# Two orders of the SBUF pools in a two-layer diffusion trunk step: the activation halves below or above the weights

## The chip, the cores and the metric

One core of a Trainium2 chip runs the whole program. The metric is the device time of one execution in microseconds: 2422.73 us before the change, the median of three runs (2418.14, 2423.43 and 2422.73).

## What is computed

The reference is one inference step of a trunk of two layers, of width 2048, over two groups of 128 tokens each (a prompt and a sample). They are computed side by side, 256 columns wide. Cut to what matters here:

```
for l in range(2):
    xp = xp + gp1 * mixer(modulate(xp, ...))     # l = 0: attention and convolution; l = 1: S5 and GQA
    xs = xs + gs1 * mixer(modulate(xs, ...))
    a  = relu(modulate(x, ...) @ w1[l])          # 2048 -> 8192
    x  = x + g2 * (a * a) @ w2[l]                # 8192 -> 2048, for both groups
y = rms_norm(x, final_norm)
```

All is float32. The shifts, scales and gates come from a modulation, which is a linear of two conditioning vectors by `ada_w`.

## The kernel before

**A linear.** Activations stand with features on the partitions: a tile `X[k]` holds 128 features of all 256 tokens. An output tile `lin` of 128 features is a sum over 16 such tiles (or another number of them). Weights arrive by DMA in pieces of 128 rows by 1024 (512 KB, 4,096 bytes on each partition) in the pool `raw` of 8 slots. ScalarE casts a piece to fp32r into `wh`, and VectorE writes what the cast lost, `raw - wh`, into `wl`; both pools have 4 slots of the piece's size. Activations are split in the same way: `put` writes the cast into the first half of a tile `hl`, and what it lost into the second half.

One piece of weights serves 8 tiles `X[k]`. For each of them `block` issues three matmuls of 256 columns: `wh` by the first half, `wh` by the second half, `wl` by the first half. So a **part** (the function `part`) is 24 matmuls, each with a weight load of its own, and a linear of 16 tiles is two parts, 48 matmuls.

**The MLP.** Both layers run the 8192 hidden features in four chunks of 16 tiles. A chunk's up stage is 16 linears by `w1` that read the 16 tiles of the modulated norm; its down stage is 16 linears by `w2` that read the chunk's 16 hidden tiles. Layer 1 runs the stages in the order up 0, up 1, down 0, down 1, up 2, down 2, up 3, down 3; layer 0 runs up and down by turns. After each up linear ScalarE writes `ms` and VectorE `mq` (the squared relu); after each down linear VectorE adds two halves to `x`. These rows mark the ends of linears in a timeline.

**Where activation halves lie.** Tiles named `hl` come from two pools. `hlp` (pool "hl", 24 slots, opened in `setup`) holds 516 numbers to a tile, 2,064 bytes, since one kind of its tiles carries two more columns; the built program sets its slots 2,080 bytes apart. `hp` (pool "hid") is opened by `mlp`, after everything in `setup`; its tiles hold 512 numbers and stand 2,048 bytes apart. Of a chunk's 16 hidden tiles the first 8 are in `hid` and the last 8 in `hlp`, except in chunk 1 of layer 1, where all 16 are in `hid`. So a down linear reads a part from `hid` and then a part from `hlp`, and an up linear reads two parts from `hlp`.

Slots of `hlp` are taken as they come free. In the built program the last part of an up linear reads slots 16, 15, 14, 13, 12, 11, 10, 9 in this order in both layers. The `hlp` part of a down linear reads 8, 1, 2, 3, 4, 5, 6, 7 in layer 0 and 12, 11, 10, 9, 4, 5, 6, 7 in layer 1.

**What sets the order.** The program is written as many strands. A first run keeps a clock for each engine and picks the order; the second builds the program in that order. The clocks don't know addresses. Loads go out on SP's queue as far ahead as `raw` has room; pieces of the modulation (`ada`, TensorE by `raw` itself, and `va` on VectorE) are woven in between.

**Where pools lie.** Pools are stacked in the order in which `setup` opens them, and the stage pools (`hid` and those of the mixers) come on top. The sum of the sizes below the stage pools is the same in either order, so stage pools don't move.

Of the kernel before, what the change touches and what calls it, by code (L numbers as in the profile page):

```python
# [48 lines left out]
class Engine:  # L49
    """An engine whose instructions are also charged to the program's clocks."""  # L50
# [27 lines left out]
class Line:  # L78
    """A strand of the program: a generator that says what its next instructions wait for."""
# [4 lines left out]
    def on_pe(self):  # L84
        """Whether its next instructions are for TensorE."""
        return callable(self.wait) and getattr(self.wait, "pe", False)
# [25 lines left out]
class Kern:  # L112
# [20 lines left out]
    # The program is many strands. A first run, that is thrown away, keeps a clock for each engine and always goes  # L133
    # on with a strand whose operands are there by then; the second run builds the program in that order, with
    # the weights loaded and split ahead of their use.
# [59 lines left out]
    def at(self, *aps):  # L195
        """When the tiles' contents are there."""
        return max([0] + [NEVER if v.tensor.name in self.held else self.at_.get(v.tensor.name, 0) for v in aps])

    def hold(self, t):
        """Not all of t is written yet."""  # L200
        self.held[t.tensor.name] = True
# [10 lines left out]
    def bulk(self, lead):  # L212
        """For work that is not urgent: the engines have come up to `lead` behind the clock of TensorE."""
        return lambda: max(self.clock["vector"], self.clock["scalar"]) + lead
# [58 lines left out]
    def get(self, *tags, on=None):  # L273
        """Waits for free slots (and for tiles), and takes them."""
        def ok():
            for t in set(tags):
                if self.live.get(t, 0) + tags.count(t) > self.cap[t]:
                    return False
            return self.when(on) + (MARGIN if "ps" in tags else 0)
        ok.pe = "ps" in tags  # L280
        yield ok
        for t in tags:
            self.live[t] = self.live.get(t, 0) + 1
# [10 lines left out]
    def setup(self):  # L294
        nc = self.nc
        self.const = self.pool("const", 1)
        self.xp = self.pool("xres", 1)
        self.hlp = self.pool("hl", 24)
        self.rawp = self.pool("raw", RAW)
        self.whp = self.pool("wh", SPLIT + 1)  # L300
        self.wlp = self.pool("wl", SPLIT + 1)
        self.work = self.pool("work", 2)
        self.ps = self.pool("ps", 1, PSUM)
        self.dram = self.pool("dram", 1, DRAM)
        pk = self.const.tile([128, _width(PACK)], F32, name="pk")
        nc.gpsimd.dma_start(pk, self.i["pack"])
        self.pk = {k: pk[:, a:b] for k, (a, b) in PACK.items()}
        self.x = self.xp.tile([128, KT, 256], F32, name="x")
        for q in range(2):
            nc.sync.dma_start(self.x[:, 8 * q:8 * q + 8], self.i["xT"][:, 8 * q:8 * q + 8])  # L310
        self.ones = self.const.tile([128, 128], F32, name="ones")
        nc.vector.memset(self.ones, 1.0)
        self.eps = self.const.tile([128, 1], F32, name="eps")
        nc.vector.memset(self.eps, EPS)
        self.ident = self.pk["ident"]
        self.condp = self.const.tile([128, KT, 32], F32, name="condp")
        nc.vector.memset(self.condp, 0.0)
        nc.scalar.activation(self.condp[:, :, 0:2], self.pk["cond"].rearrange("p (k c) -> p k c", c=2), AF.Silu)
        self.pick2 = self.const.tile([128, 2, 32], F32, name="pick2")
        nc.vector.memset(self.pick2, 0.0)  # L320
        for c in range(2):
            nc.vector.memset(self.pick2[:, c, c:c + 1], 1.0)
        self.mod, self.A, self.set_up = {}, {}, True
# [6 lines left out]
    def source(self, spec):  # L330
        """The columns of a piece, side by side."""
# [38 lines left out]
    def pump(self, upto=0):  # L370
        """Loads ahead, as far as there is room, and splits what has come (and the pieces before `upto` in any
        case)."""
# [24 lines left out]
    def slot(self, key, bufs, back=0):  # L397
        """When the slot of the next tile (or one after it) is free."""
        ring = self.rings.get(key, [])
        i = len(ring) + back - bufs  # L400
        return self.last.get(ring[i], (0, 0))[0] if 0 <= i < len(ring) else 0

    def peek(self, n, split=False):
        """When the next n raw tiles are there."""
# [5 lines left out]
    def take(self, split, *spec):  # L410
        """The next piece that has been loaded: its halves, or itself."""
# [32 lines left out]
    def there(self, X, a, b, weights=True):  # L444
        """For a wait: the tiles X[a:b], and the weights that come next."""
# [14 lines left out]
    def part(self, ps, src, X, a, b, first, last, w=None, **kw):  # L460
        """ps (+)= weight blocks a to b of a tile times X[a:b]."""
# [20 lines left out]
    def staged(self, srcs, X, width, groups, done, release=None):  # L482
        """Linears in groups: first all on the half of X that is there first."""
        n = 0
        for g in groups:
            # the first weights come before the banks are free
# [15 lines left out]
    def pairs(self, srcs, X, tags, done, cuts, between=None):  # L502
        """Linears side by side, two to a bank (of the given tags): first all on the part of X that is there first.
        done(n, ps, release) takes the tiles; between() is issued after the first part."""
# [16 lines left out]
        for i, (a, b) in enumerate(cuts):  # L521
            last = i == len(cuts) - 1
            # at the end one of each bank first: its copy out holds the bank
            for n in list(range(0, len(out), 2)) + list(range(1, len(out), 2)) if last else range(len(out)):
                ps, r = out[n]
                # the start of the first tile of a bank clears all of it
# [6 lines left out]
    def out_proj(self, src, X, done, held, between=None):  # L533
        """The tiles of an output projection, whose second half of X is there first."""
# [8 lines left out]
    def put(self, X, k, src, pool=None, slot=False):  # L543
        """X[k] = the halves of src."""
# [12 lines left out]
    def copied(self, dst, ps, note=None, release=None):  # L557
        """dst = ps, a linear's tile."""
# [10 lines left out]
    def ada(self, *pieces):  # L569
        """Two pieces (l, i, a, b) of the modulation: blocks a to b of vector i."""  # L570
# [44 lines left out]
    def ada_vector(self, n, pool):  # L615
        """Pieces of the modulation on VectorE, when it has time; TensorE only sums over the partitions."""
# [24 lines left out]
    def background(self):  # L641
        """The modulation in the order of its use: first parts of shift and scale, then theirs second."""
# [7 lines left out]
    def cuts(self, l, j):  # L650
        """The parts in which a modulated norm comes."""
        return FIRST if (l, j) == (0, 0) else ((0, 8), (8, 16))

    def mods(self, *keys):
        """For a wait: pieces of the modulation."""
        return lambda: self.at(*[self.mod[k] for k in keys]) if all(k in self.mod for k in keys) else False

# [1 line left out]
    def rstd_rows(self, sums, n, width, tag):  # L659
        """rstd of the sums in sums[:, :n] (token on the partition)."""  # L660
# [12 lines left out]
    def rstd_bcast(self, acc, width):  # L673
        """acc [128, 256]: squares summed over tiles; the rstd of each token on all partitions."""
# [20 lines left out]
    def sq_start(self, *norm):  # L695
        """The next norm's sum begins, and what doesn't wait for it."""
# [25 lines left out]
    def scales(self, l, j, a, b):  # L722
        """The factor of the modulated norm, with its gain."""
# [18 lines left out]
    # The first linears of a modulated norm don't wait for the sum over all of x: W (rstd A x + B) is  # L742
    # rstd (W A x) + W B, and B comes along as two more columns.
# [25 lines left out]
    def enter(self, l, j, srcs, groups, done):  # L769
        """The modulated norm of x; done(n, v, release) takes the first linears."""  # L770
# [36 lines left out]
    def residual(self, k, ps, l, i, summed, release=None, final=False):  # L807
        """x += gate * ps; the squares of the new x go to the next norm's sum if it has begun."""
# [17 lines left out]
    def softmax_parts(self, ps_list, scales, pool, tag, ebufs=2):  # L826
        """exp of the scaled scores (each a [128, 384] bank: prompt | sample) and the sums, per part."""
# [24 lines left out]
    def rope(self, out, src, rot, cos, sin, n, pool, tag, **kw):  # L852
        """out = src * cos + rot * sin for [128, n, 128] views."""
# [116 lines left out]
    def conv(self, gates, cins, cv, csum, mp, m2, mix):  # L970
# [21 lines left out]
        # layer norm of the convolution, silu  # L992
# [45 lines left out]
    def norm_heads(self, heads, ssq, ats, sub, m2, mix, hds):  # L1038
        """rms norm of the heads."""
# [206 lines left out]
    def gqa_scales(self, g, qss, qn, rqs, m2):  # L1246
        """The scale of each token's scores: rstd of the query, over sqrt(dim)."""
# [62 lines left out]
    def cmul(self, out_r, out_i, ar, ai, br, bi, tmp, neg_i=False):  # L1310
        """out = a * b, complex; tmp gives two scratch views of out's shape."""
# [13 lines left out]
    def s5_powers(self, kk, q1, z):  # L1325
# [4 lines left out]
        with ExitStack() as st:  # L1330
# [16 lines left out]
            # reduced angle: th - 2 pi n, with the product split so that it is exact  # L1347
# [33 lines left out]
            # k = (abar - 1) / a  # L1381
# [16 lines left out]
            # orders of powers: q1 for the chunk's state (7 - s | s), z for its output (i | 8 - i)  # L1398
# [111 lines left out]
    def s5(self, uts, mp, m2, fin, yhl):  # L1510
        """Two halves of the channels; the second one's states are prepared while the first one's are scanned."""
# [6 lines left out]
    def s5_states(self, qh, uts, mp, m2, out):  # L1518
        nc = self.nc
        u4 = range(4 * qh, 4 * qh + 4)  # L1520
        # u by (position in the chunk, channel) on the partition
# [29 lines left out]
        # states that each chunk adds  # L1551
# [38 lines left out]
    def s5_outputs(self, qh, u2, hs, mp, m2, fin, yhl):  # L1590
        nc = self.nc
        tt = nc.gpsimd.tensor_tensor
        # recurrence over the chunks (the backward half runs from the last)
# [22 lines left out]
        # outputs  # L1616
# [155 lines left out]
    def fill(self, most, goal, parts):  # L1772
        """How far the modulation pieces may run (in steps), and how far they have to within that many parts."""
# [47 lines left out]
def _channels():  # L1821
    """Order of the S5 channels: tile (qh, g4), partition (q', n)."""
# [101 lines left out]
```

## Time and profile before

| | |
|---|---|
| runs | 2418.14, 2422.73, 2423.43 us |
| profiled execution, first to last instruction | 2417.9 us |
| TensorE matmuls busy | 2331.7 us (96%) |
| VectorE, ScalarE, GpSimd busy | 1696.8, 1154.1, 173.5 us |
[...]
| DMA | 627.64 MB, mean 260 GB/s |

The span is 4.8 us under the median of the runs. Matmuls are pipelined: a matmul's row lasts some 0.28 us, while the next one starts some 0.11 us after it. What counts is therefore the distance of starts, not the length of a row. A timeline joins the two `wh` matmuls of a tile to one row (x2) and shows the `wl` matmul as the next (x1), so the distance between two `wh` rows is the time of one tile, three matmuls.

### The profile page before, as it was taken

The page shows a single profiled execution, that of the slowest core. Times are in us where ns is not written, and L with a number is a line of the kernel's source. Part 1 is how long each engine was busy: PE and PEld are TensorE (multiplying, and loading weights), DVE is VectorE, ACT ScalarE, POOL GpSimd, SP SyncE. Part 2 cuts the span into 40 slices and gives each one's busy share as a digit, 9 for nine tenths or more (in the row PEclk, how much of TensorE's full clock was granted, in tenths as well). Part 3 has the DMA queues.
Part 4 walks back from the last instruction along what each step waited for, and adds up shares of the span by engine and source line. Part 5 has one row for each costly group of instructions (what it writes and reads, how often), then busy time and mean ns, then how long its engine had stood idle before and what let it go on. Part 6 is the DMA issues. An engine that isn't in the chain of part 4 may idle for free.

```text
span 2417.9 us, 49512 instructions
## 1 busy us (share of the span) xinstructions
PE 2331.7 (96%) x20152; PEld 2134.6 (88%) x20152; DVE 1696.8 (70%) x2957; ACT 1154.1 (48%) x1894; POOL 173.5 (7%) x293
## 2 busy tenths in 40 slices
PE   6999999999999999999999978999999999999997
PEld 1788887888999999999999857799999999999997
DVE  1489985677889898887666434566998855555555
ACT  2364457465444434434455644555744333443453
POOL 0000000000111011101000236000000000000000
PEclk9999999999999999999999988999999999999998
DMA  9979987879678898879877877765587855555552
GB/s 384 339 261 325 320 312 255 293 269 317 204 265 301 300 316 299 311 263 333 281 231 249 295 281 265 270 226 181 187 295 268 273 192 193 182 191 190 184 186 94
DMA packets 179638, 627.64 MB, mean 260 GB/s; under 512 B 21377, under 2 KB 21393, under 8 KB 179153
## 3 DMA queue, kind: packets, MB, share of 16 engines
q1 hardware_dynamic: 169920, 595.67, 71.1%
q0 software_dynamic: 9488, 28.81, 3.9%
q8 instruction: 158, 2.59, 0.4%
q14 instruction: 72, 0.58, 0.1%
HBM read 602.17 MB, written 26.41 MB: 260 GB/s over the span
## 4 chain that ended last, share of the span: by engine, by line
PE 85%; DVE 3%; DMA 3%; ACT 3%; POOL 3%; issue 1%; DVEq 0%; SPq 0%; ACTq 0%; POOLq 0%
PE lin L60 76%; PE ada L60 5%; POOL rt L60 2%; DVE wl L60 1%; DMA raw<-in_ada_w 1%; POOL hs L60 1%; ACT wh L60 1%; PE m1T L60 1%; DMA raw<-m3d 1%; ACT hs L60 0%; PE ps L60 0%; DMA raw<-in_ew_in 0%; PE po L60 0%; ACT L60 0%; DMA raw<-in_w 0%
## 5 line engine op out<-in xcount | busy, mean ns | idle before, releaser
L60 PE MATMUL lin<-hl,wh 128*128 128x256 f32 (+1 forms) x11200 | 2009.6, 282 | 7.2 <-ACT wh L60 7.0
L60 PEld LDWEIGHTS lin<-hl,wh 128*128 128x128 f32 x11200 | 1715.2, 189 | 98.4 <-issue 57.4
L60 PE MATMUL lin<-hl,wl 128*128 128x256 f32 (+1 forms) x5600 | 1569.9, 280 | 12.1 <-DVE wl L60 12.1
L60 PEld LDWEIGHTS lin<-hl,wl 128*128 128x128 f32 x5600 | 1058.2, 189 | 14.9 <-DVE wl L60 14.9
L60 DVE TENSOR_TENSOR wl<-raw,wh 128x1024 fp32r<-128x1024 f32 (+1 forms) x716 | 857.2, 1206 | 278.5 <-ACT wh L60 276.8
L60 ACT CAST wh<-raw 128x1024 fp32r<-128x1024 f32 (+1 forms) x716 | 738.6, 1035 | 520.0 <-PE lin L60 273.7
L60 PE MATMUL ada<-raw,condp 128*32 128x512 f32 (+1 forms) x1408 | 186.0, 572 | 19.5 <-DMA raw<-in_ada_w 19.3
L60 DVE SCALAR_TENSOR_TENSOR x<-lin,mod,x 128x128 f32<-128x128 f32 x320 | 97.1, 345 | 102.8 <-PE lin L60 102.6
L60 DVE SCALAR_TENSOR_TENSOR va<-raw,condp,va 128x1024 f32<-128x1024 f32 x120 | 148.4, 1277 | 0.0
L60 ACT ACTIVATE ms<-lin 128x256 f32<-128x256 f32 x114 | 43.8, 384 | 155.6 <-PE lin L60 155.6
L60 ACT CAST hl<-mq 128x256 fp32r<-128x256 f32 x128 | 51.8, 406 | 96.2 <-DVE mq L60 96.2
L60 DVE SCALAR_TENSOR_TENSOR cv<-cin,pke,cv 128x256 f32<-128x256 f32 x232 | 96.5, 476 | 0.0
L60 PEld LDWEIGHTS ada<-raw,condp 128*32 128x32 f32 x1408 | 32.8, 109 | 72.0 <-DMA raw<-in_ada_w 30.5
L60 DVE SCALAR_TENSOR_TENSOR mq<-lin,ms 128x256 f32<-128x256 f32 x114 | 47.9, 420 | 61.5 <-ACT ms L60 61.3
L60 ACT ACTIVATE sq<-x 128x256 f32<-128x256 f32 x75 | 31.0, 417 | 119.1 <-DVE x L60 117.1
L60 DVE TENSOR_TENSOR hl<-mq,hl 128x256 fp32r<-128x256 f32 x128 | 53.6, 421 | 28.3 <-ACT hl L60 28.1
L60 POOL TENSOR_TENSOR x<-x,rb 128x512 f32<-128x512 f32 (+1 forms) x2 | 4.2, 2133 | 916.6 <-ACT rb L60 916.6
L60 DVE TENSOR_TENSOR acc<-acc,sq 128x256 f32<-128x256 f32 x75 | 31.8, 424 | 32.2 <-ACT sq L60 30.4
L60 DVE TENSOR_TENSOR hl<-h,hl 128x256 fp32r<-128x256 f32 (+1 forms) x112 | 45.4, 420 | 9.1 <-ACT hl L60 8.7
L60 ACT CAST hl<-h 128x256 fp32r<-128x256 f32 (+1 forms) x112 | 42.8, 402 | 12.2 <-DVE h L60 11.5
L60 POOL DMA_DIRECT2D m3d<-m x32 | 21.6, 678 | 348.3 <-DVE m L60 347.1
L60 DVE TENSOR_TENSOR w<-s5z,bc 128x576 f32<-128x576 f32 x64 | 45.5, 752 | 0.6
(281 smaller groups left out, 1167.4 us busy)
## 6 DMA issues: line engine op xcount, KB each, us to landing
raw<-in_w SPq DMA_DIRECT2D x512, 512.0 KB, 5.1
raw<-in_ada_w SPq DMA_DIRECT2D x352, 512.0 KB, 6.1
raw<-in_ew_in SPq DMA_DIRECT2D x68, 512.0 KB, 6.0
raw<-in_ow_in SPq DMA_DIRECT2D x40, 512.0 KB, 6.5
raw<-in_ada_w SPq DMA_DIRECT2D x64, 256.0 KB, 6.2
raw<-in_ew_out SPq DMA_DIRECT2D x32, 512.0 KB, 6.2
raw<-in_ow_out SPq DMA_DIRECT2D x32, 512.0 KB, 4.7
m3d<-m POOLq DMA_DIRECT2D x32, 256.0 KB, 6.3
```

Of the source, the lines that this page charges most:

```text
L60: return f(out, *a, **kw)
```

## The change

`setup` opens the pool "hl" after "work" instead of before "raw":

```
-        self.hlp = self.pool("hl", 24)
         self.rawp = self.pool("raw", RAW)
         self.whp = self.pool("wh", SPLIT + 1)
         self.wlp = self.pool("wl", SPLIT + 1)
         self.work = self.pool("work", 2)
+        self.hlp = self.pool("hl", 24)
         self.ps = self.pool("ps", 1, PSUM)
```

The rest of the diff takes out comments and the texts of functions, and leaves their lines empty, so that line numbers stay. Both programs have the same instructions in the same order on every engine, with the same waits. What differs is where six pools start, in bytes on each partition:

| pool | before | after | before, after modulo 256 |
|---|---|---|---|
| const, xres | 16512, 25920 | 16512, 25920 | 128, 64; the same |
| hl (24 x 2080) | 42304 | 117888 | 64, 128 |
| raw (8 x 4096) | 92224 | 42304 | 64, 64 |
| wh (4 x 4096) | 124992 | 75072 | 64, 64 |
| wl (4 x 4096) | 141376 | 91456 | 64, 64 |
| work | 157760 | 107840 | 64, 64 |
| hid (2048 apart) and other stage pools | 167808 | 167808 | 128, 128 |

## Rows read from the trace of the kernel before

**Rows 1.** The page: the span, and the chain's shares by engine.

```profile
span 2417.9 us, 49512 instructions
...
PE 85%; DVE 3%; DMA 3%; ACT 3%; POOL 3%; issue 1%; DVEq 0%; SPq 0%; ACTq 0%; POOLq 0%
```

**Rows 2.** Busy time in a stretch: bounds, length, each engine's microseconds, clock, DMA.

```profile
core 0: us, PE busy (x) PEld busy (x) DVE busy (x) ACT busy (x) POOL busy (x), PEclk, DMA share, GB/s
...
1922.00:2405.00 483.00, 480.35 (x4133) 480.06 (x4131) 273.89 (x366) 213.59 (x267) 0.00 (x0) 1.00 0.53 179
```

**Rows 3.** The chain that ended last, 1730 to 2410 us: start, length, what.

```profile
1922.75 479.01 PE lin L60 x4122
```

**Rows 4.** The same chain's shares by line, 600 to 1310 us (layer 0's MLP).

```profile
by line: PE lin L60 87.8%; PE ada L60 5.0%; PE m1T L60 2.0%; DMA raw<-in_w 1.3%; PE lgF L60 1.0%; DVE wl L60 0.6%; PE lgB L60 0.5%; issue 0.4%; DVE w L60 0.4%; PE adv L60 0.3%; DVE va L60 0.2%; ACT wh L60 0.1%; SPq L352 0.1%; DVE m1t L60 0.
```

**Rows 5.** Timeline of ScalarE, layer 1's up 2: start, length, what.

```profile
2048.18 0.39 ACT L60 ACTIVATE ms<-lin 128x256 f32<-128x256 f32 x1 [1.92 <-PE lin L60]
...
2070.87 0.38 ACT L60 ACTIVATE ms<-lin 128x256 f32<-128x256 f32 x1 [1.88 <-PE lin L60]
```

**Rows 6.** Timeline of VectorE, layer 1's down 1, all tiles in hid.

```profile
1960.91 0.61 DVE L60 SCALAR_TENSOR_TENSOR x<-lin,mod,x 128x128 f32<-128x128 f32 x2 [0.53 <-PE lin L60]
...
1988.11 0.61 DVE L60 SCALAR_TENSOR_TENSOR x<-lin,mod,x 128x128 f32<-128x128 f32 x2 [0.53 <-PE lin L60]
```

**Rows 7.** Timeline of VectorE, layer 1's down 2, tiles in hid and in hlp.

```profile
2144.49 0.61 DVE L60 SCALAR_TENSOR_TENSOR x<-lin,mod,x 128x128 f32<-128x128 f32 x2 [0.59 <-PE lin L60]
...
2155.59 0.61 DVE L60 SCALAR_TENSOR_TENSOR x<-lin,mod,x 128x128 f32<-128x128 f32 x2 [0.63 <-PE lin L60]
```

**Rows 8.** Timeline of TensorE, within layer 1's down 1.

```profile
1955.61 0.39 PE L60 MATMUL lin<-hl,wh 128*128 128x256 f32 x2
...
1955.95 0.39 PE L60 MATMUL lin<-hl,wh 128*128 128x256 f32 x2
...
1956.29 0.39 PE L60 MATMUL lin<-hl,wh 128*128 128x256 f32 x2
```

**Rows 9.** Timeline of TensorE, first part of layer 1's down 0, and what follows.

```profile
1864.88 0.40 PE L60 MATMUL lin<-hl,wh 128*128 128x256 f32 x2
...
1867.71 0.40 PE L60 MATMUL lin<-hl,wh 128*128 128x256 f32 x2
```

**Rows 10.** Timeline of TensorE, same stage, from the last hlp tile into hid.

```profile
1870.19 0.40 PE L60 MATMUL lin<-hl,wh 128*128 128x256 f32 x2
...
1870.55 0.39 PE L60 MATMUL lin<-hl,wh 128*128 128x256 f32 x2
...
1870.89 0.39 PE L60 MATMUL lin<-hl,wh 128*128 128x256 f32 x2
```

**Rows 11.** Timeline of TensorE, last hid part of layer 1.

```profile
2396.04 0.39 PE L60 MATMUL lin<-hl,wh 128*128 128x256 f32 x2
...
2396.38 0.39 PE L60 MATMUL lin<-hl,wh 128*128 128x256 f32 x2
```

**Rows 12.** Timeline of TensorE, first and second hid part of layer 0.

```profile
609.12 0.40 PE L60 MATMUL lin<-hl,wh 128*128 128x256 f32 x2
...
609.48 0.40 PE L60 MATMUL lin<-hl,wh 128*128 128x256 f32 x2
...
614.80 0.39 PE L60 MATMUL lin<-hl,wh 128*128 128x256 f32 x2
...
615.13 0.39 PE L60 MATMUL lin<-hl,wh 128*128 128x256 f32 x2
```

**Rows 13.** Timeline of TensorE, a hid part of layer 0 after S5 table matmuls.

```profile
852.70 0.40 PE L60 MATMUL lin<-hl,wh 128*128 128x256 f32 x2
...
853.05 0.40 PE L60 MATMUL lin<-hl,wh 128*128 128x256 f32 x2
```

**Rows 14.** Timeline of ScalarE, casts of weights in consecutive slots.

```profile
2049.37 1.04 ACT L60 CAST wh<-raw 128x1024 fp32r<-128x1024 f32 x1
2050.92 1.05 ACT L60 CAST wh<-raw 128x1024 fp32r<-128x1024 f32 x1 [0.51 <-ACT wh L60]
```

More of the change, by code (lines that the diff above doesn't have):

```diff
@@ L297, in setup @@
         self.xp = self.pool("xres", 1)
-        self.hlp = self.pool("hl", 24)
         self.rawp = self.pool("raw", RAW)
@@ L302, in setup @@
         self.work = self.pool("work", 2)
+        self.hlp = self.pool("hl", 24)
         self.ps = self.pool("ps", 1, PSUM)
```

## The prediction

> **What bounds the kernel now.** I read four views, from coarse to fine. The page's chain comes first: TensorE holds 85% of it [rows 1]. [...] In layer 0's MLP `lin` still has 87.8% of the chain [rows 4]. [...] The change moves no instruction and no wait; only a change in how long instructions take at their new addresses can alter the time. The third view, the ends of linears, tells whether addresses matter at all. In up 2, whose tiles all lie in `hlp`, four linears take 2070.87 - 2048.18 = 22.69 us [rows 5]: 5.67 us for one, 118.2 ns a matmul. In down 1, whose tiles all lie in `hid`, five take 27.20 us [rows 6]: 5.44 us, 113.3 ns. In down 2, half and half, two take 11.10 us [rows 7]: 5.55 us, 115.6 ns. The matmuls are of one shape, TensorE never waits, and still they have two paces. That is what this change can touch.
>
> The fourth view, TensorE's timeline, tells what the pace hangs on. In down 1 a tile of three matmuls takes 0.34 us again and again [rows 8]: the **quick pace**, 113.3 ns a matmul. But the first part of down 0 also reads `hid`, and its eight tiles take 1867.71 - 1864.88 = 2.83 us [rows 9], 0.354 us each, 117.9 ns a matmul: the **slow pace**. Later linears of that stage read the same eight tiles at 0.34 us [rows 10]. So it isn't the height in SBUF alone, nor the data. One address has two paces, and a run of `hid` tiles keeps the one with which it begins.
>
> **What decides the entry.** I describe a tile's start by (start - 64) modulo 256, in steps of 32 bytes; all weight slots start at 64 modulo 256 (the table of the change). `hid` tiles are all at 2. A slot s of `hlp` is at s modulo 8 before the change. The 256 is a choice: steps between starts in `hlp` parts recur for tiles 8 slots (65 x 256 bytes) apart when what was ahead of them recurs too, which I see far less well with 64 or 128. I went through all 144 parts on `hid` in the timeline.
> - Entered from an up stage, whose last tile is slot 9 (residue 1): 7 parts, all slow. The first ones of layer 0 and of layer 1 are shown [rows 9, 12].
> - Entered from a down part on `hlp`, whose last tile is slot 7 (residue 7), without a wait: 96 parts, all quick as they begin [rows 10, 12]; 5 of these in layer 0 turn slow midway after a wait.
> - Entered from `hid` itself (31 in down 1): all quick, as the first one was.
> - Begun after a wait, such as one behind S5 table matmuls: 10 parts, slow [rows 13].
>
> Quick in all: 76 of layer 1's 80 parts, the last at 2396.04 us [rows 11], and 46 of layer 0's 64, with 5 halves.
>
> **The change part by part.**
> - `raw`, `wh`, `wl` and `work` move by 49,920 bytes, 195 x 256. Casts of weights into consecutive slots take 1.04 and 1.05 us [rows 14]. ScalarE, VectorE and DMA see no new residue, and they have room [rows 2]. I take 0, within 0.01 us a cast; none of it lies on the path in layer 1.
> - `hlp` moves by 75,584 bytes, 295 x 256 + 64. So every slot's residue grows by 2: slot 7 goes from 7 to 1, slot 9 from 1 to 3. Within `hlp` nothing changes its order, and a stage's chain of tiles goes through all eight residues, so its mean should stay: 118.2 ns in an up stage [rows 5], 117.8 in a down part (2 x 115.6 less 113.3). From these two a bound: a shift by their distance, 0.4 ns, on the 13,440 matmuls that read `hlp` (the built program's 16,896 of this kind less 144 x 24) is 5.4 us either way, some 4.8 us on the path at 0.88. I take 0.
> - `hid` doesn't move against the weights modulo 256, but it is now entered from residue 1 where it was entered from 7. Every entry from 1 in the trace gave the slow pace. I take it that the parts now quick go slow. The price is 24 x (117.9 - 113.3), 0.11 us a part. Layer 1: 76 x 0.11 = 8.4 us, all on the path [rows 3]. Layer 0: 46 and 5 halves, 48.5 x 0.11 = 5.3 us, times 0.88 [rows 4], 4.7 us.
> - The 7 first parts are now entered from residue 3, which no row shows: between 0 and 7 x 0.11 = 0.8 us gained. I take the gain.
>
> [...]
>
> **Sum.** 8.4 + 4.7 - 0.8 = 12.3 us. Made against the profiled execution's 2417.9 us it gives a span of 2430; the runs' median lies 4.8 us above the span, so 2435. Some of layer 0's delay will be hidden behind loads, and an entry that climbs to residue 1 (4, 5, 6, 7 become 6, 7, 0, 1) is not quite one that falls to it (slots 12 to 9): I take off 1 us and say **2434 us**, 0.5% slower.
>
> **The rivals.**
> - *No change.* The entry hangs on a shorter period than 256, or on the direction of the chain and not on its last residue. Modulo 64 the shift by 64 is nothing at all, and so the change would do nothing to TensorE's pace. [...] Against it: a model of the steps that knows residues modulo 64 only can't tell the 7 slow entries from the 96 quick ones (1 and 7 are both odd there). For it: the two kinds differ in more than residue. Time: 2422.7, or 2418 to 2427 with half of the entries or the bound on `hlp`.
> - *Faster: height decides.* `hlp` tiles lie below the weights and never keep the quick pace, `hid` tiles above them mostly do. If lying above is what allows it, `hlp` gains what parts the stages: 3.7 us for an up stage (16 x 0.23), 1.8 for a half down stage (16 x 0.11). Layer 1: 4 x 3.7 + 3 x 1.8 = 20.2 us; layer 0: 0.88 x (4 x 3.7 + 4 x 1.8) = 19.4. The time is 2383; with half of the slots high enough, 2403. It decides from the point where some height between slot 23 (90,144) and `hid` (167,808) is crossed; the new slots lie from 117,888 to 165,728. Against it: the same `hid` address at both paces [rows 9, 10].
> - *Slower, but by less.* Only layer 1's long run in down 1 or only layer 0 flips: 3 to 6 us, 2426 to 2429.
>
> **How the numbers follow.** About 0.2% (4.8 us) is what a measurement of this kernel can tell from no change. The forecast with all or most entries flipped has 0.48, the small flip 0.12 (half of it beyond 0.2%), no change 0.22, height 0.13; 0.05 goes to a shift of `hlp` beyond its bound, mostly to a gain. Slower: 0.48 + 0.06 + 0.01 = 0.55. Same: 0.06 + 0.20 = 0.26. Faster: 0.13 + 0.04 + 0.02 = 0.19. The range runs from the low end of no change, 2416, to the forecast with `hlp` at its upper bound, 2441; it leaves out height and some of the tails, 0.18.
>
> **What would show it.** In the changed profile a linear in down 1 takes 5.66 us in place of 5.44, in down 2 some 5.66 in place of 5.55, and in up 2 still 5.67; TensorE stays at a clock of 1.00 there. If down 1 stays at 5.44, the entry was not decided by the residue. If up 2 falls towards 5.44, height or `hlp`'s distance to the weights mattered, and the forecast has the wrong sign. If casts or loads change by more than 0.05 us, the path to look at is another one.

## The result

The changed kernel takes 2436.6 us (median of four runs, 2434.5 to 2439.7); the kernel before, run beside it, 2423.1 us (2418.1 to 2424.2). The ratio is 1.006, with an interval of 1.0044 to 1.0075: slower by 0.6%. The forecast was 2434 us, and slower.

The profiled execution of after was the longest of its four (2439.7 us). Its page has the same instructions, and TensorE holds the same share of the chain as in [rows 1]:

```profile
span 2437.9 us, 49512 instructions
...
PE 85%; DMA 4%; DVE 4%; ACT 3%; POOL 3%; issue 1%; DVEq 0%; SPq 0%; ACTq 0%; POOLq 0%
```

The stretch of after that answers to [rows 2] (bounds, length, busy microseconds of PE, PEld, DVE, ACT and POOL, clock, DMA share):

```profile
1936.00:2419.00 483.00, 483.00 (x4096) 483.00 (x4095) 273.33 (x358) 211.28 (x263) 0.00 (x0) 1.00 0.53 178
```

The granted clock is 1.00 as before and the DMA share 0.53 as before. TensorE starts 4096 matmuls in 483.00 busy microseconds (117.9 ns each), where it started 4133 in 480.35 (116.2 ns). So neither the clock nor the loads made the difference. The chain of after in the same place, as [rows 3] (start, length, what):

```profile
1843.14 90.63 PE lin L60 x768
...
1935.89 486.35 PE lin L60 x4122
```

The first of these two pieces before the change, which [rows 3] leaves out:

```profile
1831.01 89.62 PE lin L60 x768
```

The same 4122 matmuls take 486.35 us in place of 479.01, 7.34 us more, with no wait among them; the 768 ahead of them take 1.01 us more. Which ones, the ends of linears show. Timeline of ScalarE in up 2 of after, as [rows 5]:

```profile
2065.30 0.38 ACT L60 ACTIVATE ms<-lin 128x256 f32<-128x256 f32 x1 [1.90 <-PE lin L60]
...
2087.99 0.39 ACT L60 ACTIVATE ms<-lin 128x256 f32<-128x256 f32 x1 [1.86 <-PE lin L60]
```

Four up linears take 22.69 us, exactly as before. Timeline of VectorE in down 1 and down 2 of after, as [rows 6, 7]:

```profile
1974.83 0.61 DVE L60 SCALAR_TENSOR_TENSOR x<-lin,mod,x 128x128 f32<-128x128 f32 x2 [0.64 <-PE lin L60]
...
2003.10 0.61 DVE L60 SCALAR_TENSOR_TENSOR x<-lin,mod,x 128x128 f32<-128x128 f32 x2 [0.64 <-PE lin L60]
...
2161.71 0.61 DVE L60 SCALAR_TENSOR_TENSOR x<-lin,mod,x 128x128 f32<-128x128 f32 x2 [0.60 <-PE lin L60]
...
2173.03 0.61 DVE L60 SCALAR_TENSOR_TENSOR x<-lin,mod,x 128x128 f32<-128x128 f32 x2 [0.64 <-PE lin L60]
```

Five linears of down 1 take 28.27 us, 5.65 each (5.44 before); two of down 2 take 11.32 us, 5.66 each (5.55 before). All of the loss is in parts on `hid`. TensorE's timeline in down 0 of after, as [rows 9, 10], from the first `hid` tile to the first tile of the next part, and then from the last `hlp` tile into `hid` again:

```profile
1877.02 0.40 PE L60 MATMUL lin<-hl,wh 128*128 128x256 f32 x2
...
1879.85 0.40 PE L60 MATMUL lin<-hl,wh 128*128 128x256 f32 x2
...
1882.31 0.40 PE L60 MATMUL lin<-hl,wh 128*128 128x256 f32 x2
...
1882.67 0.40 PE L60 MATMUL lin<-hl,wh 128*128 128x256 f32 x2
...
1883.03 0.40 PE L60 MATMUL lin<-hl,wh 128*128 128x256 f32 x2
...
1883.38 0.40 PE L60 MATMUL lin<-hl,wh 128*128 128x256 f32 x2
```

The first part takes 2.83 us for eight tiles, the slow pace as before. The part entered from `hlp` at 1882.67 goes on at 0.36 and 0.35 us a tile, where [rows 10] has 0.34 us.

To follow this through all runs I count tiles of three matmuls in TensorE's timeline, by distances of starts, and call a tile **quick** under 346 ns (tiles with a wait in them are left out; 304 of the 4480 `hlp` tiles have 258 columns, and none of those is quick). Of 1113 `hid` tiles 977 were quick before and 17 are after; their mean went from 341.6 to 353.5 ns. The `hlp` tiles have 354.2 and 354.5 ns, with 51 and 45 quick.

A table by stage, worked out from the timelines of one execution each (us; the marks are the first and last start of a matmul on `hid` in layer 0, the first in layer 1, and the start of the last matmul of the program's linears):

| kernel | layer 0 starts | layer 0, down 0 to down 3 | to layer 1's down 0 | from there to the end |
|---|---|---|---|---|
| before | 609.1 | 698.0 | 557.7 | 536.6 |
| after | 611.9 | 703.4 | 561.7 | 544.9 |
| low_64 | 608.7 | 703.2 | 558.7 | 544.9 |
| high_192 | 609.9 | 698.1 | 561.2 | 536.6 |
| flat_2 | 607.1 | 701.0 | 559.6 | 544.0 |
| kick_all | 609.7 | 691.8 | 553.1 | 526.9 |
| kick_67 | 605.0 | 690.1 | 548.8 | 526.4 |

The last matmul of a linear starts 20.5 us later in the profiled execution of after. Of these, 5.4 arise in layer 0's MLP and 8.3 in layer 1's from its first down part on. The other 6.8 (2.8 ahead, 4.0 between) are in the mixers, and low_64, whose `hlp` has the residues of after, shows only 0.6 there in sum, while high_192, with the residues of before, shows 4.3. So I put them down to this execution, and 13.7 us to the change; that is a reading of single executions, not shown by a run of its own; the medians differ by 13.5.

### The profile page after: what moved, and what is told of

It reads as the page before. It is cut to its first block, busy times and chain, and to the rows that moved or that the text cites. A ratio compares the mean times of both kernels' runs of the same rounds, so it can differ in the third digit from the quotient of the medians.

```text
span 2437.9 us, 49512 instructions
## 1 busy us (share of the span) xinstructions
PE 2351.4 (96%) x20152; PEld 2152.7 (88%) x20152; DVE 1698.9 (70%) x2957; ACT 1153.1 (47%) x1894; POOL 173.3 (7%) x293
## 4 chain that ended last, share of the span: by engine, by line
PE 85%; DMA 4%; DVE 4%; ACT 3%; POOL 3%; issue 1%; DVEq 0%; SPq 0%; ACTq 0%; POOLq 0%
PE lin L60 75%; PE ada L60 5%; POOL rt L60 2%; DVE wl L60 1%; DMA raw<-in_ada_w 1%; POOL hs L60 1%; ACT wh L60 1%; DMA raw<-in_ew_in 1%; DMA raw<-m3d 1%; PE m1T L60 1%; ACT hs L60 0%; PE ps L60 0%; DVE hl L60 0%; PE po L60 0%; ACT L60 0%
## 5 line engine op out<-in xcount | busy, mean ns | idle before, releaser
L60 DVE TENSOR_TENSOR wl<-raw,wh 128x1024 fp32r<-128x1024 f32 (+1 forms) x716 | 859.0, 1207 | 280.9 <-ACT wh L60 278.5
L60 ACT CAST wh<-raw 128x1024 fp32r<-128x1024 f32 (+1 forms) x716 | 737.6, 1034 | 523.1 <-PE lin L60 271.4
L60 POOL TENSOR_TENSOR x<-x,rb 128x512 f32<-128x512 f32 (+1 forms) x2 | 4.2, 2132 | 927.8 <-ACT rb L60 927.8
```

Of the source, the lines that this page charges most:

```text
L60: return f(out, *a, **kw)
```

## The experiments

All times of before below were taken on the same chip as the run they stand beside. The rows named "x" are VectorE's additions to `x` in one 32 us window of down 1: six linears with two instructions each, so the distance from the first start to the last is five linears and some 0.28 us. 27.5 is the quick pace (5.44 us a linear) and 28.5 the slow one (5.65). The three numbers ahead of it in such a row are the shortest, median and longest addition in ns.

### Shift alone, height alone

**low_64**: `hlp` stays low, and is shifted as against the weights.

```
+        self.pool("pada", 1).tile([128, 16], F32, name="pada")
         self.hlp = self.pool("hl", 24)
+        self.pool("padb", 1).tile([128, 48], F32, name="padb")
         self.rawp = self.pool("raw", RAW)
```

> The pool of the activation halves lies below raw, wh, wl and work as in the kernel before, but 64 bytes higher; 192 bytes of padding behind it keep raw, wh, wl, work and hid at their old starts modulo 256. Theory of the residue: every hlp slot stands 2 steps of 32 bytes further against the weights, as in the changed kernel, so hid parts are entered from residue 1 and run at the slow pace: a linear of down 1 takes 5.66 us, the time is 2433 to 2439 us. Rival, height: hlp lies below the weights as before, so the quick pace stays: 5.44 us, 2420 to 2425 us. Rival, period of 64 bytes: as height, 5.44 us and 2420 to 2425 us.

**high_192**: `hlp` lies high, and is shifted back.

```
         self.work = self.pool("work", 2)
+        self.pool("pada", 1).tile([128, 48], F32, name="pada")
+        self.hlp = self.pool("hl", 24)
+        self.pool("padb", 1).tile([128, 16], F32, name="padb")
```

> The pool lies above raw, wh, wl and work as in the changed kernel, but 192 bytes higher, so that every slot has the residue modulo 256 against the weights that it had before the change; 64 bytes behind it keep hid at its start modulo 256. Theory of the residue: quick entries again, a linear of down 1 in 5.44 us, 2420 to 2426 us. Rival, height (hlp above the weights is what costs): 5.66 us, 2433 to 2439 us.

Measured: low_64 2433.8 us, ratio 1.0051 (1.0039 to 1.0063). high_192 2422.2 us, ratio 1.0004 (0.9993 to 1.0014), against 2421.1 us of before. The longest piece of the chain and the x row of low_64:

```profile
1929.36 486.35 PE lin L60 x4122
...
L60 DVE SCALAR_TENSOR_TENSOR x<-lin,mod,x x12: 341/347/353, 1968.3 to 1996.8; 128x128 f32<-128x128 f32 x12
```

and of high_192:

```profile
1927.04 479.01 PE lin L60 x4122
...
L60 DVE SCALAR_TENSOR_TENSOR x<-lin,mod,x x12: 340/346/352, 1965.2 to 1992.7; 128x128 f32<-128x128 f32 x12
```

Low with the shift is after to a hundredth of a microsecond (486.35), high without it is before (479.01). Of the `hid` tiles 3 and 977 are quick. Height does nothing that these runs can tell; the 64 bytes do all of it. The theories of height and of a period of 64 bytes fall. In every run of this document the weight slots start at 64 modulo 256, so the runs can't tell whether the start of an activation tile counts by itself or by its distance to the weights; "residue" names both.

### Another shift

**low_128**: as low_64, with 128 bytes ahead of `hlp` and 128 behind it.

```
+        self.pool("pada", 1).tile([128, 32], F32, name="pada")
         self.hlp = self.pool("hl", 24)
+        self.pool("padb", 1).tile([128, 32], F32, name="padb")
```

> The pool of the activation halves lies low as in the kernel before, but 128 bytes higher, with 128 bytes of padding behind it, so every hlp slot stands 4 steps of 32 bytes further against the weights and everything else stays modulo 256. If a period of 128 bytes decides, nothing changes: a linear of down 1 in 5.44 us, 2418 to 2426 us. If the period is 256, down parts are entered from residue 3 in place of 7; the first parts that the changed kernel enters from residue 3 were slow, so down 1 takes 5.66 us and the time is 2431 to 2437 us.

Measured: 2432.0 us, ratio 1.0041 (1.0027 to 1.0054). The x row:

```profile
L60 DVE SCALAR_TENSOR_TENSOR x<-lin,mod,x x12: 341/347/351, 1968.9 to 1997.4; 128x128 f32<-128x128 f32 x12
```

Slow, so 128 is no period. But it is not all slow: 207 `hid` tiles are quick. All 7 first parts are, entered from residue 5 in layer 0 and 7 in layer 1, and so are 20 of the 51 parts of layer 0 that are entered from residue 3 without a wait. One last residue gives both paces here. That speaks against my theory as I had put it. Nor must the residues rise: the four first parts of layer 0 are entered by way of 4, 3, 2, 1, 0, 7, 6, 5.

### One residue for all tiles

**p2080_ctl** and **p2304_0**: room is made by fewer `raw` slots and fewer of the mixer's work tiles (`bufs` of these tiles goes from 5 to 4 too, not shown); p2304_0 spends it on wider `hlp` tiles.

```
-RAW = 8
+RAW = 7
...
-            self.cap.update(t1k=5, qs=4, gh=2, qr=2, PTd=1, big=1, u2=2)
+            self.cap.update(t1k=4, qs=4, gh=2, qr=2, PTd=1, big=1, u2=2)
```

and, in p2304_0 alone, in both places that make the tiles (one is shown):

```
-        t = (pool or self.hlp).tile([128, 512 if pool else 516], F32R, name="hl", tag="hl")
+        t = (pool or self.hlp).tile([128, 512 if pool else 576], F32R, name="hl", tag="hl")
```

> The kernel before with 7 raw tiles in place of 8 and 4 in place of 5 small work tiles in layer 1's mixer, hlp tiles 2080 bytes apart and low as before. All theories: the pace of the matmuls is that of the kernel before, 5.44 us for a linear of down 1; fewer tiles ahead cost 0 to 15 us, 2422 to 2438 us. It is the control for the wider pitch.

> hlp tiles 2304 bytes apart in place of 2080, so that all 24 slots start at the same residue 0 modulo 256, that of the weights; to make room there are 7 raw tiles in place of 8, and 4 in place of 5 small work tiles in layer 1's mixer, which its control p2080_ctl has too. Theory of the residue: the changing residue from tile to tile is what keeps hlp parts at some 118 ns a matmul, so with one residue hlp can hold the quick pace: 13,440 matmuls x 4.6 ns x 0.88 = 54 us less than its control at best. If the pace is only kept from the entry, and entries after a wait are slow, everything stays slow: 117.8 ns for hlp and hid alike, and the time is that of its control plus 8 to 13 us. Rival, height or no role of the residue: the time of its control within 3 us.

Measured: p2080_ctl 2452.0 us, ratio 1.0126 (1.0111 to 1.0142); p2304_0 2479.2 us, ratio 1.024 (1.0226 to 1.0254), 27 us above its control. Both missed what I expected, and the order of instructions differs from that of before in both. TensorE's timeline of p2304_0, eight tiles of an `hlp` part:

```profile
2094.99 0.40 PE L60 MATMUL lin<-hl,wh 128*128 128x256 f32 x2
...
2097.87 0.40 PE L60 MATMUL lin<-hl,wh 128*128 128x256 f32 x2
```

2.88 us for eight, 0.36 us a tile: with residue 0 throughout, `hlp` has a third pace, 360 ns, the tenth and ninetieth percentile both 360. A constant residue is no cure; it depends on which (means of 346.2 to 359.9 ns in the table of the next section).

The control says more. It has the residues of before, and yet its x row would read slow: in down 1 a linear takes 5.65 us. Freed slots came in another order, and its down parts in layer 1 read residues 4, 3, 2, **0**, 4, 5, 6, 7, where before read 4, 3, 2, **1**, 4, 5, 6, 7. TensorE's timeline of three `hid` parts in a row, each entered from residue 7: of the first two the first tile and the tile behind the eighth, of the third its first two tiles:

```profile
1970.17 0.40 PE L60 MATMUL lin<-hl,wh 128*128 128x256 f32 x2
...
1973.00 0.40 PE L60 MATMUL lin<-hl,wh 128*128 128x256 f32 x2
...
1975.84 0.39 PE L60 MATMUL lin<-hl,wh 128*128 128x256 f32 x2
...
1978.56 0.39 PE L60 MATMUL lin<-hl,wh 128*128 128x256 f32 x2
...
1981.40 0.40 PE L60 MATMUL lin<-hl,wh 128*128 128x256 f32 x2
...
1981.76 0.40 PE L60 MATMUL lin<-hl,wh 128*128 128x256 f32 x2
```

2.83 us for eight tiles, then 2.72, then a first tile of 0.36: slow, quick, slow. In layer 1, 24 entries from 7 are quick and 21 slow, without a wait ahead. Where no wait lies between one `hid` part and the next they alternate: behind a slow part 18 of 18 are quick, behind a quick one 21 of 21 slow. So the last residue alone doesn't decide; the residues ahead of it and the pace of the `hid` part before them count too. What of this control's 31 us is due to its 7 `raw` slots and what to its work tiles I didn't take apart.

### Three constant residues at a time

**mix_a**, **mix_b**, **mix_c**: p2304_0 with an offset for each tile. The same code runs with three tables (the lists are written short here).

```
+STEPS = [4] * 8 + [2] * 8 + [6] * 8                        # mix_a
+STEPS = [1] * 8 + [3] * 8 + [5] * 8                        # mix_b
+STEPS = [2, 6] * 4 + [0, 4] * 4 + [7] * 8                  # mix_c
...
+    def hl_tile(self):
+        r = 8 * STEPS[self.n_slot % 24]
+        self.n_slot += 1
+        return self.hlp.tile([128, 576], F32R, name="hl", tag="hl")[:, r:r + 516]
```

> p2304_0 with a fixed offset in each slot, so that most tiles of one part have the same residue: 4 in the first half of an up stage, 2 in the second, 6 in most down parts on hlp. In p2304_0 every tile entered from a tile of the same residue 0 took 360 ns. If any constant residue costs the same, as far as only change of residue matters, all parts on hlp take 360 ns a tile again and the time is that of p2304_0, 2470 to 2485 us. If the residue against the weights sets the pace, the residues differ: residue 2 gives 353 or 340 ns as in hid, 4 and 6 something else between 340 and 360, and the time lies between 2420 and 2475 us.

> As mix_a, with residues 1, 3 and 5 in the three groups. If a constant residue costs 360 ns a tile whatever it is: 2470 to 2485 us. If the residue against the weights sets the pace, the three groups have three paces between 340 and 360 ns, and hid is entered from 5 in most down parts, which no run has shown: quick (5.44 us a linear) or slow (5.66 us), with 8 us between them.

> As mix_a, with residues 2 and 6 in turn in the first half of an up stage, 0 and 4 in turn in the second, and 7 in most down parts on hlp, so that hid is entered from residue 7 as in the kernel before, but by way of a run of equal residues. If the last residue alone decides, the entries are quick: 5.44 us a linear in down 1. If the climb or fall of the residues ahead of it decides, 5.66 us. Time between 2420 and 2485 us.

One execution of each: 2459.2, 2464.5 and 2460.8 us. Mean time of an `hlp` tile of 256 columns that follows one of its own residue, from TensorE's timelines (0 from p2304_0, the others from the three runs above):

| residue | 0 | 1 | 2 | 3 | 4 | 5 | 6 | 7 |
|---|---|---|---|---|---|---|---|---|
| ns for three matmuls | 359.7 | 351.5 | 353.3 | 359.9 | 356.1 | 353.3 | 346.2 | 354.5 |
| tiles | 3480 | 1421 | 1241 | 1240 | 1421 | 528 | 531 | 531 |
| of these quick | 0 | 0 | 7 | 0 | 0 | 0 | 287 | 0 |

So the mean does differ with the residue, by up to 14 ns a tile. But a mean can mix two paces: at residue 6 more than half of the tiles are quick. Of mix_a's 85 runs at residue 6 (four tiles or more of 256 columns with no wait inside) 47 are quick from their third tile on, 15 of 22 among those behind a wait. TensorE's timeline of mix_a, such a run from its first tile to the tile behind its eighth:

```profile
1957.25 0.40 PE L61 MATMUL lin<-hl,wh 128*128 128x256 f32 x2
...
1959.98 0.40 PE L61 MATMUL lin<-hl,wh 128*128 128x256 f32 x2
```

2.73 us for eight. In these runs of equal residues only 2 and 6 were ever quick, and no residue always. The entries into `hid` without a wait are nearly all slow here: 42 of 42 from a run of residue 6 in mix_a, 42 of 42 from a run of 5 in mix_b, and 39 of 42 from a run of 7 in mix_c: last tile 7, and no quick pace. What was special about before was then not the 7 alone, but the 7 together with what was read ahead of it.

### Keeping the quick pace

**scratch_ctl**: room of another kind, which moves nothing modulo 256. In the built program all pools start 5,376 (21 x 256) bytes lower than before.

```
-    nc = bacc.Bacc("TRN2", target_bir_lowering=False, num_devices=1)
+    nc = bacc.Bacc("TRN2", target_bir_lowering=False, num_devices=1, dynamic_dma_scratch_size=11008)
```

> [...] It is the control for the next two. Theory of the residue: nothing changes, a linear of down 1 takes 5.44 us, 2418 to 2426 us. [...]

**flat_2**, **kick_all**, **kick_67**: this room, with wide tiles whose offset goes by their place `k` in the sixteen (the lists are written short again).

```
+ACTS = HID = [2] * 16                          # flat_2
+ACTS = HID = [2] * 12 + [4, 5, 6, 7]           # kick_all
+ACTS = HID = [2] * 14 + [6, 7]                 # kick_67
...
+    def hl_tile(self, step):
+        return self.hlp.tile([128, 576], F32R, name="hl", tag="hl")[:, 8 * step:8 * step + 516]
...
-        t = (pool or self.hlp).tile([128, 512 if pool else 516], F32R, name="hl", tag="hl")
+        t = pool.tile([128, 512], F32R, name="hl", tag="hl") if pool else self.hl_tile((HID if hid else ACTS)[k])
```

> The room from the control is spent on hlp tiles 2304 bytes apart, all with residue 2, that of the hid tiles; 8 raw tiles and all work tiles stay, raw, weights, work and hid lie where they lay before. If a run of equal residues only keeps the pace with which it began, and runs that begin after a wait are slow, then everything stays slow: 353 ns for three matmuls in hlp and in hid, 5.66 us a linear in every stage of both MLPs; hid loses 12 us, hlp gains 1 to 2 ns a tile (up to 6 us), 2425 to 2436 us. If equal residues of 2 alone gave the quick pace, 340 ns a tile everywhere, 2375 to 2395 us.

> As flat_2, but the last four of each sixteen hlp tiles have residues 4, 5, 6, 7, rising as they do ahead of the quick entries of the kernel before; the other twelve have 2. If the rise to 7 brings TensorE into the quick pace and a run of equal residues keeps it, then 12 of 16 tiles of an up stage run at 340 ns and all hid tiles do: an up linear takes 5.50 us in place of 5.67, a down linear 5.48, the same in the linears of the mixers, and the time falls by 25 to 40 us to 2380 to 2398 us. If the entry needs more than those four residues (a run of eight, or the falling run ahead of it), everything stays slow as in flat_2: 2425 to 2440 us.

> As kick_all, but only the last two of each sixteen hlp tiles leave residue 2, with 6 and 7. If the step from 6 to 7 and back to 2 alone brings the quick pace, 14 of 16 tiles of a linear run at 340 ns; against kick_all two tiles of each linear go from some 351 to 340 ns, 350 linears x 2 x 11 ns = 8 us, of which some 7 us are on the path: 2386 to 2392 us. If the rise from 4 is needed, nothing is quick: hid and hlp at 353 ns a tile as in flat_2, 5.66 us a linear in down 1, 2425 to 2435 us.

| kernel | median us | ratio to before | interval | quick `hid` tiles | quick `hlp` tiles |
|---|---|---|---|---|---|
| scratch_ctl | 2420.4 | 1.0001 | 0.9991 to 1.001 | 977 of 1113 | |
| flat_2 | 2431.3 | 1.0044 | 1.0027 to 1.0061 | 44 of 1113 | 142 of 4027 |
| kick_all | 2396.5 | 0.989 | 0.9873 to 0.9908 | 981 of 1113 | 1700 of 4027 |
| kick_67 | 2392.8 | 0.9888 | 0.9872 to 0.9905 | 1023 of 1113 | 2132 of 4031 |

The x rows of scratch_ctl, flat_2, kick_all and kick_67, in this order:

```profile
L60 DVE SCALAR_TENSOR_TENSOR x<-lin,mod,x x12: 341/347/352, 1961.2 to 1988.7; 128x128 f32<-128x128 f32 x12
```

```profile
L62 DVE SCALAR_TENSOR_TENSOR x<-lin,mod,x x12: 340/348/353, 1965.4 to 1993.9; 128x128 f32<-128x128 f32 x12
```

```profile
L62 DVE SCALAR_TENSOR_TENSOR x<-lin,mod,x x12: 341/346/351, 1949.5 to 1977.0; 128x128 f32<-128x128 f32 x12
```

```profile
L62 DVE SCALAR_TENSOR_TENSOR x<-lin,mod,x x12: 340/346/351, 1938.7 to 1966.2; 128x128 f32<-128x128 f32 x12
```

27.5, 28.5, 27.5, 27.5 us: the control is quick, the flat kernel is slow, and both kernels with a rise in each sixteen are quick. ScalarE's timeline in up 2 of flat_2 and then of kick_all, four linears each:

```profile
2055.84 0.39 ACT L62 ACTIVATE ms<-lin 128x256 f32<-128x256 f32 x1 [1.90 <-PE lin L62]
...
2078.45 0.39 ACT L62 ACTIVATE ms<-lin 128x256 f32<-128x256 f32 x1 [1.85 <-PE lin L62]
```

```profile
2036.59 0.38 ACT L62 ACTIVATE ms<-lin 128x256 f32<-128x256 f32 x1 [1.82 <-PE lin L62]
...
2058.51 0.38 ACT L62 ACTIVATE ms<-lin 128x256 f32<-128x256 f32 x1 [1.78 <-PE lin L62]
```

22.61 us, 5.65 a linear, against 21.92 us, 5.48 a linear (5.67 in [rows 5]): with residue 2 and a rise at the end of each sixteen, `hlp` tiles hold the quick pace too. The longest piece of the chain of kick_all, the same 4122 matmuls as in [rows 3], is 479.01 - 470.12 = 8.9 us shorter:

```profile
1911.68 470.12 PE lin L62 x4122
```

The order of instructions on every engine is that of before in all four kernels. So 1.1% is had from starts of tiles alone, and both kernels with a rise are faster than the one before; flat_2, with the same room and no rise, is not. kick_all is 23.8 us under the before on its chip: inside the range of times expected, but just short of the 25 to 40 us. 42% of its `hlp` tiles became quick, not 75%. In up 2 (2031 to 2120 us), where TensorE doesn't wait, it is 75%; in layer 0's MLP (600 to 1310 us) 39%, and before 600 us 19%. There TensorE waits: in the trace of before its weight loads for `lin` stand idle for 27.7 us in that MLP and for 44.7 us from 115 to 600 us, against 0.0 us from 1922 to 2405 us. That the waits end the quick runs is read from these shares, and no run isolates it. In kick_67 all 102 entries into `hid` without a wait are quick (94 of 103 in kick_all, 4 of 103 in flat_2). So behind tiles of residue 2 the step from 6 to 7 and back to 2 is enough, though the `hid` tile at the entry still takes 342 ns on the mean and the tiles at 6 and 7 some 353 and 356 ns. It isn't enough everywhere: p2080_ctl has the same step behind 4, 3, 2, 0, 4, 5 and 21 slow entries. The median of kick_67 is 1 us above the range expected, and the 7 us by which it should beat kick_all are not shown: 0.9888 and 0.989 can't be told apart.

## Why the prediction was right

- **What bounds.** Right. The sum took layer 1's loss as all on the path [rows 3], and the window and the chain of after show it paid in full: 483.00 of 483.00 us busy, and 7.34 us more in the chain piece.
- **`raw`, weights and `work` cost nothing.** Right: the mean cast into `wh` takes 1034 ns (1035 before), VectorE's subtraction into `wl` 1207 (1206). That ScalarE and VectorE see no new residue was not quite so: they write the `hl` tiles, whose starts moved by 64 modulo 256. It cost nothing: 406 and 421 ns for the two halves of a hidden tile, before and after.
- **`hlp` itself costs nothing on the mean.** Right: four linears of up 2 take 22.69 us in both kernels. The bound of 5.4 us either way wasn't needed.
- **Quick parts turn slow.** Right in size: layer 1 lost 8.3 us from its first down part to the end (8.4 in the sum), layer 0 5.4 us (4.7 in the sum, at 0.88 of 5.3). So layer 0 hid none of its loss as far as these executions tell; the factor 0.88 from [rows 4] was too low.
- **The seven first parts.** Wrong, by the 0.8 us taken as a gain: the rows at 1877.02 and 1879.85 show 2.83 us, slow as before. The text had them all entered from residue 1. Only layer 0's four are. In layer 1 the last up part ahead of down 0, 2 and 3 reads slots 16, 15, 14, 13, 8, 1, 2, 3, as the addresses of the built program show, and not 16 down to 9 as the description of the kernel before has it. So these three were entered from residue 3 before the change, and slow, and are entered from 5 after it. Looked up, the slow entries from 3 would have left little ground for a gain in layer 0's four; for an entry from 5 there was no row.
- **The 1 us taken off** had no ground in the end: 8.4 + 5.3 from the sum, with nothing hidden and nothing gained, is the 13.7 found in the stages.
- **The reason behind the entry** was right in its kind and too narrow. That where `hlp` starts modulo 256 decides, not height, is shown by low_64 and high_192, which separate what the change had joined. That the residue of the *last* tile decides is refuted by low_128, p2080_ctl and mix_c. That the rule of the last residue gave the right forecast is in part luck: its evidence for residue 1 was four parts entered by a fall (4, 3, 2, 1), while after the change the entries come by 6, 7, 0, 1, which no row had shown. In low_128 entries by 4, 5, 6, 7, 0, 1, 2, 3, just as new, went both ways in layer 0.
- **The rivals.** Height is refuted, periods of 64 and 128 bytes are refuted, and the small flip too: both layers flipped, 977 quick tiles to 17.

**What stays open.** No run tells what holds the pace, or why the step from 6 to 7 and back to 2 starts the quick one behind tiles of 2. No run moves the weights modulo 256, so the part of their start is open too. The traces show only that the pace has a memory: a run at residue 2 goes on at the pace at which it began (down 1 from end to end: 256 of 256 tiles quick before, 340 ns on the mean, and none of 256 after, 353 ns; every x row above has one of the two paces), and nearly every `hid` part that begins after a wait is slow (10 of 10 before, 8 of 10 after); at residue 6 that is not so (15 of 22 runs behind a wait are quick from their third tile on in mix_a).

## What to carry to other kernels

Where TensorE never waits and equal matmuls still have more than one distance of starts, sort them by the starts of their operands modulo 256, and by what was read ahead of them: padding of 64 bytes cost 0.5% here, and a layout that brings the quick pace on purpose gained 1.1%. A change that only moves pools is not neutral until the starts modulo 256 have been compared (this one cost 13.5 us); a twin that moves the pool but keeps the residue, and one that keeps the pool and moves the residue, settle it in two runs. And a control that alters how slots come free can change the pace as well (5.65 us a linear in down 1 of p2080_ctl, 5.44 before), so compare the order of residues as well as the count of instructions.

## What the runs showed of the hardware that I had not expected

- Matmuls of 256 columns in fp32r, each with a weight load, ran steadily at 113.3, 117.8 or 120.0 ns (the first two in down 1 before and after, at a granted clock of 1.00), by the starts of the activation tiles and what went before. The 120.0 ns are those of 3480 tiles in p2304_0, with no spread between the tenth and ninetieth percentile, at a mean granted clock of 0.988.
- Parts with the same eight addresses and the same eight residues ahead of them took turns at 0.340 and 0.353 us a tile, each the opposite of the part before it, 39 times out of 39 (p2080_ctl).
- Tiles at residue 6 could be quick with no rise ahead of them, also behind a wait (mix_a, 15 of 22 runs).
- All pools 5,376 bytes lower, with `dynamic_dma_scratch_size=11008`, cost nothing here: 2420.4 us, 1.0001 (0.9991 to 1.001) in scratch_ctl.
